# First modulation of a diffusion trunk: weights by pairs of feature blocks, three projection blocks beside them

## The chip, the cores and the metric

The kernel runs on one core of one Trainium2 chip. The metric is device time in microseconds (us) of one execution; lower is better. The engines are named as the profile names them: PE (TensorE, matrix products), PEld (its weight loads), DVE (VectorE), ACT (ScalarE), POOL (GpSimd) and SP (SyncE, which issues most loads). An engine works through its own instructions in a fixed order, and so does the queue of loads on SP.

## The reference

One sample, 512 latent tokens and 256 context tokens, 1024 features, two layers. The change lies in the very beginning of layer 0: the modulation vectors are computed from the conditioning, the tokens are normed and modulated, and the first input projection starts.

```python
silu_c = jax.nn.silu(c)
silu_cc = jax.nn.silu(c_ctx)
m_l = (silu_c @ w_mod[i] + b_mod[i])[:, None, :]       # w_mod[i]: 1024 x 6144
m_c = (silu_cc @ w_mod[i] + b_mod[i])[None, None, :]
sh1, sc1, g1, sh2, sc2, g2 = jnp.split(m_l, N_MOD, axis=-1)
hl = modulate(x, norm1_g[i], sh1, sc1)                 # rmsnorm(x) * (1 + sc1) + sh1
hc = modulate(ctx, norm1_g[i], csh1, csc1)
z  = h @ a_w_in                                        # 1024 -> 1440, for hl and for hc
# then two kinds of attention on parts of z, output projection, MLP; layer 1: Hyena, MLP
```

Only sh1 and sc1 (the first 2048 of 6144 columns of w_mod) are needed for the first projection. The other four parts are computed later in the background.

## The kernel before

Activations are kept transposed: features on the 128 partitions, in KD = 8 blocks, tokens along the free axis (`xnT`, `hl`). To reach near float32 precision, an operand is split into a rounded part and the rest (`hi`, `lo`; `split_w` does that to weights with one ACT and one DVE instruction), and a product is three matmuls (`mm3`: hi x hi, L109; hi x lo, L110; lo x hi, L111). One output block of the projection for the 512 latent tokens is thus 8 x 3 matmuls into one PSUM tile `sm`. The pool of those tiles (psB) has four buffers; the larger `big` tiles (psA) have two.

**Set-up** (`build`, L1297 to L1321). `conditioning` makes the silu of both conditioning vectors. `mod_start` (L272) loops over the eight blocks k of 128 input features: it loads a token tile of x (only for k < 4), then rows k*128 to k*128+127 of w_mod, columns 0 to 2047, as one load of 1 MiB with rows of 8 KiB (`wm`, three buffers). `norm0` norms the token tile and turns it with PE into xnT. Four matmuls (L289) add the block's product to one PSUM tile, in which row 32n+v holds columns 512n to 512n+511 for vector v (latent or context). The sum over k is complete only after the last load. `part` loads the weights of the first two output blocks of a_w_in (columns 672 to 927) in two halves. `vectors` (L225) loads biases and gains over the ACT queue and turns them into columns (`Acol`, `Bcol`, `Ccol`). `mod_finish` (L324) copies the sums out, turns them with four transposes (L331) and makes shift and scale columns `shsc`. `modulate0` (L344) then computes for each of the eight feature blocks hi on ACT (L349), the unrounded product on DVE (L351, one buffer `m0t`) and lo on DVE (L352). `context0` (L294) loads, norms and turns the two context tiles into `xcT`.

**Input projection** (`attn_in`, L457). Twelve output blocks follow each other: four of the grouped queries (`gq`, blocks j = 0 to 3, latent tokens only), then keys, values and the latent-attention parts, most of them for latent and context tokens. Blocks 0 and 1 run side by side over k. After each gq block, ACT takes the square (L515) and a scaled copy `gq0` (L517; one buffer), and DVE rotates it (L436 to L439). Block 0 stays in gq0 until it has been split for two heads (L723, L724). `context` modulates the context tokens. The generator `hidden` runs the filter network of layer 1 in between. After each block `block_done` calls `tick(3)`.

**Background.** `mod_chunks` (L354) computes the remaining four parts of the modulation on DVE: for each part eight loads of 512 KiB (`modw`, three buffers), eight multiply-adds (L372, L374), a transpose (L377) and a sum (L378). One step runs per tick, 37 steps in all, and the results are needed after the attention.

**Order.** A scheduler orders the instructions of each engine and of the SP queue when the program is built. It keeps their order in the program as priority, but lets a later instruction go first where it expects an earlier one to be still waiting. `keep_in_program_order` fixes an instruction in place. Tiles of a pool that is closed are overwritten by later pools as soon as their last reader is done. Pools grow from both ends of the memory (`side="right"`).

## Time and profile before

| what | value |
|---|---|
| median of 3 runs | 1534.65 us (1530.81 to 1539.14) |
| the profiled execution | 1532.22 us, span 1530.4 us |
| PE busy | 1431.5 us (94%) |
| DVE busy | 1107.9 us (72%) |
| ACT busy | 676.2 us (44%) |
| POOL busy | 294.1 us (19%) |
| DMA | 186.05 MB, mean 122 GB/s |

The span is the time from the first to the last instruction in the profiled execution. Busy shares are means over a span with several stages; the stage that is changed is its first 110 us. PE's busy time counts matmuls as overlapping intervals, so it is near the whole of a stage also where PE has to wait in between.

### The profile page before, as it was taken

Reading aid. Unit: us, or ns where it says so; the run is one execution under the profiler, and the core shown is the slowest. Engines: PE = TensorE matmul, PEld = TensorE weight load, DVE = VectorE, ACT = ScalarE, POOL = GpSimd, SP = SyncE. Lnnn points to the kernel's source line nnn. Section 1 sums busy time; section 2 is a strip of 40 time slices with the busy share of each in tenths; the row PEclk is TensorE's granted clock in tenths of the full one; section 3 lists DMA queues with packets and bytes.
Section 4 is the critical chain, followed back from the end, with each engine's and each line's share of the span. In section 5 each row is a group of like instructions: output and inputs, shape, how many; then the busy total and the mean of one; then the engine's idle time right before and its main releaser. Section 6 shows DMA issues by size and latency. Waiting matters only on the chain. (4 is left out here: it accounts for less than half of the span.)

```text
span 1530.4 us, 19652 instructions
## 1 busy us (share of the span) xinstructions
PE 1431.5 (94%) x7516; PEld 1191.7 (78%) x7516; DVE 1107.9 (72%) x1645; ACT 676.2 (44%) x1075; POOL 294.1 (19%) x245
## 2 busy tenths in 40 slices
PE   6798899999999998989999999999989999999998
PEld 2476687888887777878788977787778888888888
DVE  3999899877788989789765659897977434343454
ACT  3544587666644345345434444435234323132342
POOL 0000144322100322232220035634330000000001
PEclk8899899999999999999999999999999999999999
DMA  9655301211547655554334333321231232323331
GB/s 322 213 175 182 87 1 41 53 42 51 159 146 230 209 179 175 172 196 165 119 112 146 106 117 110 104 90 56 83 110 56 86 108 88 105 90 103 94 127 56
DMA packets 135435, 186.05 MB, mean 122 GB/s; under 512 B 16536, under 2 KB 118685, under 8 KB 132270
## 3 DMA queue, kind: packets, MB, share of 16 engines
q1 hardware_dynamic: 133168, 174.62, 35.3%
q0 software_dynamic: 1440, 9.70, 1.8%
q8 instruction: 59, 0.97, 0.3%
q10 hardware_dynamic: 734, 0.48, 0.1%
q14 instruction: 34, 0.28, 0.1%
HBM read 171.67 MB, written 10.49 MB: 119 GB/s over the span
## 5 line engine op out<-in xcount | busy, mean ns | idle before, releaser
L125 ACT CAST whi<-wraw 128x1024 fp32r<-128x1024 f32 (+2 forms) x203 | 195.9, 972 | 346.3 <-PE sm L110 311.0
L126 DVE TENSOR_TENSOR wlo<-wraw,whi 128x1024 fp32r<-128x1024 f32 (+2 forms) x195 | 235.8, 1212 | 121.1 <-ACT whi L125 108.3
L111 PE MATMUL sm<-h_hi,wlo 128*128 128x512 f32 (+1 forms) x720 | 273.6, 381 | 5.9 <-DVE wlo L126 5.9
L109 PE MATMUL sm<-h_hi,whi 128*128 128x512 f32 (+1 forms) x720 | 276.5, 387 | 2.6 <-ACT h_hi L425 1.7
L110 PE MATMUL sm<-h_lo,whi 128*128 128x512 f32 (+1 forms) x720 | 273.6, 381 | 0.7 <-DVE h_lo L426 0.7
L109 PE MATMUL sm<-mHhi,whi 128*128 128x512 f32 (+1 forms) x640 | 225.9, 354 | 2.4 <-ACT mHhi L169 2.3
L110 PE MATMUL sm<-mHlo,whi 128*128 128x512 f32 (+1 forms) x640 | 223.6, 350 | 3.4 <-DVE mHlo L172 3.4
L111 PE MATMUL sm<-mHhi,wlo 128*128 128x512 f32 (+1 forms) x640 | 223.2, 349 | 0.3 <-DVE wlo L126 0.2
L843 DVE SCALAR_TENSOR_TENSOR xT<-sm,mod,xT 128x256 f32<-128x256 f32 (+1 forms) x128 | 78.1, 614 | 131.8 <-PE sm L111 131.6
L111 PEld LDWEIGHTS sm<-h_hi,wlo 128*128 128x128 f32 x720 | 135.3, 188 | 34.6 <-DVE wlo L126 8.9
L109 PEld LDWEIGHTS sm<-h_hi,whi 128*128 128x128 f32 x720 | 134.8, 189 | 31.1 <-ACT h_hi L425 2.5
L110 PEld LDWEIGHTS sm<-h_lo,whi 128*128 128x128 f32 x720 | 135.8, 189 | 27.9 <-DVE h_lo L426 1.3
L110 PEld LDWEIGHTS sm<-mHlo,whi 128*128 128x128 f32 x640 | 121.7, 190 | 20.1 <-DVE mHlo L172 4.6
L109 PEld LDWEIGHTS sm<-mHhi,whi 128*128 128x128 f32 x640 | 121.6, 190 | 20.0 <-ACT mHhi L169 3.4
L111 PEld LDWEIGHTS sm<-mHhi,wlo 128*128 128x128 f32 x640 | 121.6, 190 | 16.7 <-DVE wlo L126 1.3
L647 POOL TENSOR_SCALAR prob<-prob,smx 128x768 f32<-128x768 f32 x64 | 60.4, 943 | 301.6 <-DVE smx L646 248.1
L374 DVE SCALAR_TENSOR_TENSOR modacc<-modw,silu,modacc 128x1024 f32<-128x1024 f32 x70 | 93.3, 1333 | 22.1 <-DMA modw<-in_w_mod 21.4
L937 POOL TENSOR_TENSOR Kout<-kE,kO 128x512 f32<-128x512 f32 x32 | 46.3, 1471 | 311.7 <-DVE kE L1073 190.9
L1257 POOL TENSOR_TENSOR facc<-facc,fsq 128x256 f32<-128x256 f32 x12 | 9.5, 792 | 386.7 <-ACT fsq L1255 386.7
L169 ACT CAST mHhi<-ms 128x512 fp32r<-128x512 f32 x64 | 39.6, 621 | 84.2 <-DVE ms L883 84.1
L1134 POOL TENSOR_TENSOR zx<-zx,zt 128x384 f32<-128x384 f32 x64 | 64.4, 1028 | 60.5 <-ACT zt L1132 59.3
L645 ACT ACTIVATE prob<-big,smx,qry 128x768 f32<-128x768 f32 x64 | 63.7, 996 | 12.3 <-DVE smx L643 9.6
(455 smaller groups left out, 2889.9 us busy)
## 6 DMA issues: line engine op xcount, KB each, us to landing
wraw<-in_mlp_w SPq DMA_DIRECT2D x67, 1024.0 KB
modw<-in_w_mod SPq DMA_DIRECT2D x80, 512.0 KB
wraw<-in_h_w_in SPq DMA_DIRECT2D x12, 1024.0 KB
wm<-in_w_mod SPq DMA_DIRECT2D x8, 1024.0 KB
kd<-Kout POOLq DMA_DIRECT2D x8, 1024.0 KB, 4.5
Kin<-kd SPq DMA_DIRECT2D x8, 1024.0 KB
wraw<-in_a_w_out SPq DMA_DIRECT2D x9, 512.0 KB
wraw<-in_a_w_in SPq DMA_DIRECT2D x4, 1024.0 KB
```

The costliest lines, as they stand in the source:

```text
L109: mm(ps, w.hi, x.hi, start=first, stop=False)
L110: mm(ps, w.hi, x.lo, start=False, stop=False)
L111: mm(ps, w.lo, x.hi, start=False, stop=last)
L125: pin(nc.scalar.copy(hi, r3))
L126: pin((lo_eng or nc.vector).tensor_tensor(out=lo, in0=r3, in1=f(hi), op=ALU.subtract))
L169: nc.scalar.copy(dst.hi, src)
L374: nc.vector.scalar_tensor_tensor(out=acc, in0=w, scalar=s, in1=acc, op0=ALU.mult, op1=ALU.add)
L645: nc.scalar.activation(out=p, in_=sf, func=AF.Exp, bias=sm[:, 1:2], scale=sc, accum_out=sm[:, 2:3])
L647: nc.gpsimd.tensor_scalar(out=p, in0=p, scalar1=sm[:, 3:4], scalar2=1.0, op0=ALU.mult, op1=ALU.mult)
L843: nc.vector.scalar_tensor_tensor(out=xt, in0=ps, scalar=gcol[:, d:d + 1], in1=xt, op0=ALU.mult, op1=ALU.add)
L937: tt = lambda e, o, x, y, op: e.tensor_tensor(out=o, in0=x, in1=y, op=op)
L1134: nc.gpsimd.tensor_tensor(out=t[:, o0:o0 + n], in0=t[:, o0:o0 + n], in1=b[:, i0:i0 + n], op=ALU.add)
```

## The change

Five things change, all within the first stage.

1. `mod_start` and `mod_finish` go; `mod_block(j)` takes their place, called for j = 0 to 3. Each call computes shift and scale of the feature blocks 2j and 2j+1 alone, over all 1024 input features. It loads 256 columns of shift and 256 of scale in eight loads of 256 KiB (two tiles `wm` of four loads; rows of 1 KiB). Four matmuls run beside each other on four groups of 32 PE columns, each with its own k; the second half adds to the first. So four partial sums lie at partitions 0, 32, 64, 96, and four small matmuls with `sel` (a matrix that picks partitions 0 mod 32 and 1 mod 32) add them up and turn them at once.
2. `modulate0` is called for two feature blocks at a time, right after their `mod_block`, and 18 matmuls follow: two feature blocks by three output blocks of three matmuls.
3. Three output blocks (j = 0, 1, 2) thus run along with the modulation instead of two after it. Their three PSUM tiles `ps3` are handed to `attn_in`, which computes only block j = 3 itself. The weights of blocks 2 and 3 come as one load `raw1` behind the first pair; block 3's half is split in `attn_in`.
4. All four token tiles of x are loaded first (`n0x` has four buffers instead of three), and `vectors` runs ahead of them.
5. The context loads and the first three background loads keep their place in the program, behind the modulation's weights; the pool `modp` of the background is opened after the set-up pool is closed, not before it.

```diff
-    def mod_start(self, tp, w0):
...
+    def mod_block(self, tp, j):
         nc, a = self.nc, self.a
+        both = self.big()
+        ps, pt = both[:, 0], both[:, 1, 0:8]
+        src = a["w_mod"][0].rearrange("(h k p) (m c) -> h p k m c", p=P, h=2, c=D)
+        for h in range(2):
+            w = tp.tile([P, 4, 2, 256], F32, name="wm", bufs=4)
+            for k in range(4):
+                nc.sync.dma_start(out=w[:, k], in_=src[h, :, k, 0:2, 256 * j:256 * j + 256])
+            for k in range(4):
+                nc.tensor.matmul(ps[32 * k:32 * k + 32], self.silu2[:, 4 * h + k], w[:, k].rearrange("p m c -> p (m c)"),
+                                 start=(h == 0), stop=(h == 1))
+        rows = tp.tile([P, 512], F32, name="modrow", bufs=2)
+        nc.vector.tensor_copy(rows[:, 0:256], ps[:, 0:256])
+        nc.scalar.copy(rows[:, 256:512], ps[:, 256:512])
+        for i in range(4):
+            nc.tensor.matmul(pt[:, 2 * i:2 * i + 2], rows[:, i * P:(i + 1) * P], self.sel, start=True, stop=True)
+        t = self.shsc[:, :, :, 2 * j:2 * j + 2]
+        pick = lambda ap, m: ap.rearrange("p (m j) -> p m j", m=m)[:, :, 2 * j:2 * j + 2].unsqueeze(1).broadcast_to([P, 2, m, 2])
+        nc.vector.tensor_tensor(out=t, in0=pt.rearrange("p (m e v) -> p v m e", m=2, e=2), in1=pick(self.Acol[:, 0:16], 2), op=ALU.add)
+        nc.vector.scalar_tensor_tensor(out=t[:, :, 1:2], in0=t[:, :, 1:2], scalar=1.0, in1=pick(self.n1g(0), 1),
+                                       op0=ALU.add, op1=ALU.mult)
     def context0(self, tp):
         for t in (4, 5):
+            xt = tp.tile([P, D], F32, name="n0x", bufs=4)
+            self.tc.keep_in_program_order(self.nc.sync.dma_start(out=xt, in_=self.a["ctx"][0, (t - 4) * P:(t - 3) * P]))
             self.norm0(tp, t, xt)
...
-    def mod_finish(self, tp):
...
-    def modulate0(self, h, v, x, tp, name):
-        nc = self.nc
-        for k in range(KD):
-            sh, g = self.shsc[v][:, k:k + 1], self.shsc[v][:, 8 + k:9 + k]
+    def modulate0(self, h, v, x, tp, name, ks=range(KD)):
+        nc = self.nc
+        for k in ks:
+            sh, g = self.shsc[:, v, 0, k:k + 1], self.shsc[:, v, 1, k:k + 1]
             nc.scalar.activation(out=h.hi[:, k], in_=x[:, k], func=AF.Identity, bias=sh, scale=g)
-            t = tp.tile([P, S], F32, name=name, bufs=1)[:, 0:x.shape[2]]
+            t = tp.tile([P, S], F32, name=name)[:, 0:x.shape[2]]
             nc.vector.tensor_scalar(out=t, in0=x[:, k], scalar1=g, scalar2=sh, op0=ALU.mult, op1=ALU.add)
             nc.vector.tensor_tensor(out=h.lo[:, k], in0=t, in1=f(h.hi[:, k]), op=ALU.subtract)
...
-                    nc.sync.dma_start(out=w, in_=a["w_mod"][l, k * P:(k + 1) * P, m * D:(m + 1) * D])
+                    load = nc.sync.dma_start(out=w, in_=a["w_mod"][l, k * P:(k + 1) * P, m * D:(m + 1) * D])
+                    if (l, m) == (0, 2) and k < mb:
+                        self.tc.keep_in_program_order(load)
...
-    def attn_in(self, hl, hc, w0, gp, ip, tp, context):
+    def attn_in(self, hl, hc, pss_w, raw1, gp, ip, tp, context):
         nc, a = self.nc, self.a
         w_in = a["a_w_in"][0]
         flat = lambda ps: ps.rearrange("p b n -> p (b n)")[:, 0:L]
-        ws = self.weights([w_in[:, i:j] for i, j in ((928, 1184), (1184, 1440), (384, 640), (640, 672), (0, 256), (256, 384))], KD)
+        cols = ((1184, 1440), (384, 640), (640, 672), (0, 256), (256, 384))
+        ws = self.weights([w_in[:, i:j] for i, j in cols], KD, self.fetch(w_in[:, 1184:1440], KD, 256))
         pss = self.sm()
         self.gq = []
         for c in range(2):
-            w = next(ws) if c else w0
-            both = [] if c else [self.sm() for _ in range(2)]
-            for k in range(KD):
-                for ps, wm in zip(both, w):
-                    self.mm3(ps, wm[:, k], hl[:, k], k == 0, k == KD - 1)
             for m in range(2):
                 j = 2 * c + m
-                if both:
-                    ps = both[m]
+                if j < 3:
+                    ps = pss_w[j]
                 else:
+                    w = self.split_w(raw1[:, :, 128:256])
                     ps = self.sm()
                     for k in range(KD):
-                        self.mm3(ps, w[m][:, k], hl[:, k], k == 0, k == KD - 1)
-                        if m and k == 2:
+                        self.mm3(ps, w[:, k], hl[:, k], k == 0, k == KD - 1)
+                        if k == 2:
...
+                with pool(name="setup", bufs=1, side="right") as tp:
+                    self.conditioning(tp)
+                    self.vectors(tp)
+                    hl, hc = (Split(hp0.tile([P, KD, n], F32R, name=nm + "_hi"), hp0.tile([P, KD, n], F32R, name=nm + "_lo"))
+                              for nm, n in (("hl", S), ("hc", C)))
+                    self.xcT = self.wp.tile([P, KD, C], F32, name="wraw")
+                    self.xnT = tp.tile([P, KD, S], F32, name="xnT")
+                    self.shsc = self.const.tile([P, 2, 2, KD], F32, name="shsc")
+                    for t in range(4):
+                        xt = tp.tile([P, D], F32, name="n0x", bufs=4)
+                        nc.sync.dma_start(out=xt, in_=self.rows(a["x"])[t])
+                        self.norm0(tp, t, xt)
+                    w3 = self.weight(a["a_w_in"][0][:, 672:928], KD, 256)
+                    raw1 = tp.tile([P, KD, 256], F32, name="wraw1")
+                    ps3 = [self.sm() for _ in range(3)]
+                    for j in range(4):
+                        self.mod_block(tp, j)
+                        if j == 0:
+                            nc.sync.dma_start(out=raw1, in_=a["a_w_in"][0][:, 928:1184].rearrange("(k p) n -> p k n", p=P))
+                            w3.append(self.split_w(raw1[:, :, 0:128], tp))
+                        self.modulate0(hl, 0, self.xnT, tp, "m0t", (2 * j, 2 * j + 1))
+                        for k in (2 * j, 2 * j + 1):
+                            for ps, w in zip(ps3, w3):
+                                self.mm3(ps, w[:, k], hl[:, k], k == 0, k == KD - 1)
+                    self.context0(tp)
                 mod_es = E(ExitStack())
                 self.modp = mod_es.enter_context(pool(name="modp", bufs=1))
                 self.mod_bufs = 3
                 self.bg = [self.mod_chunks(0, (2, 3, 4, 5), m0)]
-                with pool(name="setup", bufs=1, side="right") as tp:
-                    self.conditioning(tp)
-                    hl, hc = (Split(hp0.tile([P, KD, n], F32R, name=nm + "_hi"), hp0.tile([P, KD, n], F32R, name=nm + "_lo"))
-                              for nm, n in (("hl", S), ("hc", C)))
-                    self.xcT = self.wp.tile([P, KD, C], F32, name="wraw")
-                    raw, w0 = self.wp.tile([P, KD, 256], F32, name="wraw"), []
-                    def part(m):
-                        nc.sync.dma_start(out=raw[:, :, 128 * m:128 * m + 128],
-                                          in_=a["a_w_in"][0][:, 672 + 128 * m:800 + 128 * m].rearrange("(k p) n -> p k n", p=P))
-                        if m == 0:
-                            w0.append(self.split_w(raw[:, :, 0:128]))
-                    self.mod_start(tp, part)
-                    self.vectors(tp)
-                    fin = self.mod_finish(tp)
-                    next(fin)
-                    w0.append(self.split_w(raw[:, :, 128:256], pin=self.tc.keep_in_program_order))
-                    self.modulate0(hl, 0, self.xnT, tp, "m0t")
-                    next(fin)
-                    self.context0(tp)
                 ip_es = E(ExitStack())
                 ip = ip_es.enter_context(pool(name="ip", bufs=1, side="right"))
                 gp_es = E(ExitStack())
                 gp = gp_es.enter_context(pool(name="gp", bufs=1, side="right"))
                 with pool(name="inp", bufs=1) as tp:
-                    self.attn_in(hl, hc, w0, gp, ip, tp, lambda: self.modulate0(hc, 1, self.xcT, tp, "rpsh"))
+                    self.attn_in(hl, hc, ps3, raw1, gp, ip, tp, lambda: self.modulate0(hc, 1, self.xcT, tp, "rpsh"))
                 mod_es.close()
             self.pairs = []
             op_es = E(ExitStack())
```

Left out are the bodies of mod_start and mod_finish, which stand above, and two helper signatures.

## Rows read from the trace of the kernel before

**Rows 1.** Stretches: length, each engine's busy time, PE's granted clock, DMA share, GB/s.
```profile
0.00:42.00 42.00, 26.49 (x136) 11.31 (x136) 13.39 (x39) 15.05 (x23) 0.20 (x4) 0.85 0.91 330
42.00:130.00 88.00, 74.58 (x336) 53.01 (x336) 87.53 (x138) 43.07 (x63) 0.00 (x0) 0.95 0.64 201
130.00:190.00 60.00, 49.89 (x226) 37.77 (x227) 51.44 (x81) 30.67 (x50) 6.38 (x7) 0.86 0.34 98
```

**Rows 2.** Timeline, last weight block to first modulation: start, length, engine, line, operation.
```profile
37.85 1.94 PE L289 MATMUL sm<-wm,silu 128*32 128x512 f32 x8 [2.34 <-DMA wm<-in_w_mod]
...
41.90 0.55 DVE L351 TENSOR_SCALAR m0t<-xnT,shsc 128x512 f32<-128x512 f32 x1
```

**Rows 3.** Groups of DVE, 42 to 106 us: busy time, mean ns of one, idle.
```profile
L126 DVE TENSOR_TENSOR wlo<-wraw,whi 128x1024 fp32r<-128x1024 f32 x5 | 6.1, 1216 | 0.0
L352 DVE TENSOR_TENSOR hl_lo<-m0t,hl_hi 128x512 fp32r<-128x512 f32 x8 | 5.5, 689 | 0.1
L351 DVE TENSOR_SCALAR m0t<-xnT,shsc 128x512 f32<-128x512 f32 x8 | 4.4, 545 | 0.0
...
L322 DVE COPY wraw<-big 128x1024 f32<-128x1024 f32 x2 | 2.5, 1226 | 0.0
...
L311 DVE TENSOR_SCALAR n0n<-n0x,n0s 128x1024 f32<-128x1024 f32 x2 | 1.5, 752 | 0.0
...
L179 DVE SCALAR_TENSOR_TENSOR n0s<-n0s 128x1 f32<-128x1 f32 x2 | 0.3, 156 | 0.0
```

**Rows 4.** The DMA engines, 0 to 38 us.
```profile
DMA packets 4404, 12.22 MB, mean 322 GB/s; under 512 B 411, under 2 KB 2672, under 8 KB 3378
```

**Rows 5.** Stretches of 5 us in the load stage, columns as above.
```profile
0.00:5.00 5.00, 0.00 (x0) 0.00 (x0) 0.45 (x3) 1.16 (x1) 0.20 (x4) 1.00 0.65 192
...
10.00:15.00 5.00, 4.75 (x26) 2.53 (x18) 1.96 (x6) 2.46 (x4) 0.00 (x0) 1.00 1.01 417
15.00:20.00 5.00, 4.39 (x28) 2.41 (x29) 2.89 (x7) 2.46 (x4) 0.00 (x0) 1.00 0.80 254
...
35.00:40.00 5.00, 2.45 (x12) 0.20 (x8) 1.37 (x2) 1.04 (x1) 0.00 (x0) 0.50 1.06 363
```

**Rows 6.** A stretch that loads rows of 1 KiB alone (wraw of mlp_w).
```profile
1140.00:1145.00 5.00, 5.00 (x44) 5.00 (x43) 2.61 (x5) 0.71 (x2) 0.00 (x0) 1.00 1.05 355
```

**Rows 7.** Groups of DVE, 0 to 42 us.
```profile
L327 DVE COPY modrow<-sm 128x256 f32<-128x256 f32 x1 | 0.4, 425 | 2.3 <-PE sm L289 2.3
...
L337 DVE TENSOR_TENSOR shsc<-sm,Acol 128x16 f32<-128x16 f32 x2 | 0.3, 170 | 1.2 <-PE sm L331 1.2
L339 DVE SCALAR_TENSOR_TENSOR shsc<-shsc,Acol 128x8 f32<-128x8 f32 x2 | 0.2, 166 | 0.0
```

**Rows 8.** A group of PE in 0 to 42 us, and L289 in the timeline.
```profile
L331 PE MATMUL sm<-cst,modrow 128*128 128x128 f32 x4 | 1.1, 431 | 0.5 <-DVE modrow L327 0.5
```
```profile
25.86 1.06 PE L289 MATMUL sm<-wm,silu 128*32 128x512 f32 x8
```

**Rows 9.** Timeline of PE: end of output block 2, end of block 3.
```profile
77.49 0.62 PE L111 MATMUL sm<-hl_hi,wlo 128*128 128x512 f32 x2
...
83.49 0.39 PE L110 MATMUL sm<-hl_lo,whi 128*128 128x512 f32 x1
83.72 0.39 PE L111 MATMUL sm<-hl_hi,wlo 128*128 128x512 f32 x1
```

**Rows 10.** Timeline of SP: the first background loads.
```profile
34.47 10.72 SPq L369 DMA_DIRECT2D modw<-in_w_mod  x4
```

**Rows 11.** Timeline of ACT: square and scaled copy of blocks 0 and 1.
```profile
63.82 0.60 ACT L515 ACTIVATE sqS<-sm 128x512 f32<-128x512 f32 x1 [0.73 <-PE sm L111]
64.31 0.68 ACT L517 ACTIVATE gq<-sm,Ccol 128x512 f32<-128x512 f32 x1
...
74.02 0.69 ACT L517 ACTIVATE gq<-sm,Ccol 128x512 f32<-128x512 f32 x1 [1.65 <-DVE qs L724]
```

**Rows 12.** Waits of SP, 0 to 42 us; and a load in the chain that ended last.
```profile
SPq L285 <- DMA vC<-in_h_f_b: 5.8, 2, 5.5
```
```profile
1131.39 3.34 DMA wraw<-in_h_w_out
```

46 lines of the change are left out of this document (5 added, 41 removed).

## The prediction

> **What bounds the kernel now.** The change sits in the first 110 us of a span of 1530.4 us, so I read that stretch alone. First, the busy time by stretch [rows 1]. Up to 42 us VectorE (DVE) works 13.39 us and is idle for 28.6, while the DMA engines are 91% busy at 330 GB/s: this stage is bound by loads. From 42 to 130 us it turns over: DVE is busy 87.53 of 88 us, TensorE (PE) 74.58, the DMA 64%. From 130 to 190 us DVE is idle for 8.5 us. So the reader is to see two stages with two limits, loads and then DVE, and PE is the limit of neither although its share over the whole span is the largest.
>
> Second, where the first stage ends, in the timeline [rows 2]. The modulation's eighth and last weight block lets its matmuls start at 37.85; the sums are copied out and turned, and the first modulation op on DVE starts at 41.90. From the data to modulation it is 4.05 us, and nothing of the eight feature blocks can be modulated before.
>
> Third, what DVE does from 42 us on [rows 3]: the latent modulation (L351 and L352, 8 times each), weight splits (L126), context norm (L311, L322), rotations, and the background modulation (L374). The background steps are issued three per finished output block, and they are all needed later.
>
> **The change part by part.** The ledger is kept on DVE, because from 42 us on a microsecond is won only where DVE's idle time is removed. I take as milestone the moment at which all eight feature blocks are modulated and three output blocks' weights split.
>
> Before: 13.39 us of work by 42, of which 0.10 belongs to the first m0t; then 8 x 0.545 + 8 x 0.689 = 9.87 for modulation [rows 3], less that 0.10, and two more splits at 1.216 = 2.43. Together 25.6 us. DVE has no idle time after 42, so this content corresponds to 42 + 12.2 = 54.2 us; whatever else ran in between is work that need not be done again.
>
> After: the last weight pair must land first. Before moved 12.22 MB in its first 38 us [rows 4], 322 GB/s. Up to the last pair the new order moves x 2.10, the modulation's weights 8.39, two 1 MiB loads of a_w_in 2.10 (before: one) and constants 0.40, in all 12.99 MB: 40.3 us. Then the same 4.05 us to modulation (the four sum-and-turn matmuls with sel stand in for the four transposes of L331) and two feature blocks at 0.545 + 0.689: milestone at 40.3 + 4.05 + 2.47 = 46.9 us. Gain 54.2 - 46.9 = **7.3 us**.
>
> Bounds of that load time: the best and worst 5 us stretch of the load stage gave 417 and 254 GB/s [rows 5]. With 0.96 MB moved by 5 us, the last pair lands between 33.9 and 52.4 us, so this term lies between a gain of 13.7 and a loss of 4.8. I stay near the mean, because rows of 1 KiB alone, which is the new shape of these loads, ran at 355 GB/s [rows 6].
>
> Small DVE and ACT work: the row copy, addition and gain (L327, L337, L339: 0.425, 0.170, 0.166 each [rows 7]) run four times: 3.0 us instead of 1.1. The extra 1.9 us lie ahead of the milestone, where 25.6 + 1.9 = 27.5 us of work have 46.9 us: cost 0, and 1.9 if that cover were gone. ACT's four copies of the second half lie beside them.
>
> PE: the same 64 records of L289, 16 turning matmuls instead of 4 (0.43 each at the low clock [rows 8]), and 72 matmuls of three output blocks at 0.23 us pitch [rows 9] = 16.5 us, 12.4 of which now lie before the last pair lands. Per pair PE needs 2 x 1.06 + about 1.1 + 18 x 0.23 = 7.4 us at full clock, while a pair's 2.10 MB take 6.5 us: PE may be a little behind at the end. The bound is 0 to 4 us; I take **-1**, as a 1 MiB load (3.3 us) also lies between the pairs and lets PE catch up.
>
> Context: its two loads are now held behind the weights; their 1.05 MB land some 3.3 us after the last pair. Its norm costs DVE 0.75 + 1.23 + 0.6 us a tile [rows 3]. The first tile's start may fall into DVE's 4 us of waiting for the last sums: **+1.3** (0 to 2.6).
>
> Background: its first load was issued at 34.47 [rows 10] and now follows ctx, the rotary table and one a_w_in load (2.62 MB, 8 us), and its buffers share memory with set-up tiles that are freed only as the three blocks end. So DVE has only context work from 46.9 to about 53 us, and part of that waits for PE: a hole of 0 to 4 us, and I take **-1**. SP's queue is in order: a background load that waits for memory also holds the next a_w_in load behind it, but that is needed only after the fourth block.
>
> PE ahead of DVE: three blocks end at about 50 us, where before ends its third at 78.1 [rows 9]. That lead is not the gain. The next step on ACT (L517) needs gq0, which has one buffer that DVE's rotation frees: of the two blocks that PE had closed together by 63.8 the first had its turn at 64.31 and the second only at 74.02, released by DVE [rows 11]. PE will thus be held by DVE. What the lead does remove is some of the 8.5 us of DVE idleness between 130 and 190 us: **+2** (0 to 8.5).
>
> Sum: 7.3 - 1 + 1.3 - 1 + 2 = **8.6 us**. The profiled execution took 1532.2 (its span and 1.8 around it), which gives 1523.6; the median of the runs stands 2.4 higher, which gives 1526. I predict 1525.
>
> A rule that speaks against the change: eight loads of 1 MiB become 32 of 256 KiB. The Trainium skill, "DMA: Bandwidth & Descriptors", section "Bandwidth", asks to batch to 1 MiB or more, and its fit (2.0 us and bytes over 436 GB/s, measured on the GpSimd path) would give 2.6 us to each small load, 83 us for 32 end to end as an estimate from that page. No row shows loads of this size in a chain; the first rival prices it from rows.
>
> **The rivals.**
> A, slower: the small loads don't fill the DMA engines. Place: SP's queue, from 8 to 40 us. SP already waited 5.8 us there for small loads of another queue to land, and a 512 KiB load that was waited for alone took 3.34 us, 157 GB/s [rows 12]. At that rate the 8.39 MB take 53.4 us instead of 26.0, the milestone moves by 27, and 8.6 becomes a loss of 19: 1551. It turns slower by more than 0.5% where these loads fall below 8.39 / (26.0 + 16.3) = 198 GB/s. Against it: many loads are in flight together, and 355 GB/s for 1 KiB rows [rows 6].
> B, faster: PE's lead counts. Four blocks end at about 57 us instead of 84.1 [rows 9], and if DVE can push the background steps behind the attention's own work, as much as 26 us: 1506 to 1515. Against it: DVE is busy 87.53 of 88 us [rows 1], and the background steps stand ahead in the program.
> C, slower too, through PE: it falls to the low clock between the pairs, as between 35 and 40 us before (granted 0.50 of 2.4 GHz, so 1.2 [rows 5]). Then a pair costs PE 2 x 1.94 [rows 2] + 1.7 + 18 x 0.46 = 14 us against 6.5 of loading. The first pair is there at (2.10 + 1.05 + 2.10 + 0.40) / 0.322 = 17.5 us, and the milestone comes at 17.5 + 3 x 14 + 4.05 + 2.47 = 66 us, 12 later than 54.2: 1544. It decides from about 10 us a pair. Against it: the clock was full from 10 to 20 us while PE was busy for 9.1 of 10 [rows 5].
> D, it does not do what it says: the pairs are read early, but modulation still starts only after the last, because norms, Acol or PE's order hold it. All 9.87 us then follow 44.4: 54.3, no gain, 1532.
>
> **How the numbers follow.** Forecast 0.60 (1518 to 1532 by its bounds), A 0.08, B 0.12, C 0.08, D 0.12. A measurement of this kernel can tell about 0.5% (7.7 us) from no change. The forecast's 8.6 lies just beyond that, so some two thirds of its chance (0.40) go to faster and the rest to the same; B is faster (0.12); D is the same and a part of C, whose 14 us a pair is the dearest case; A and the rest of C, with the 0.02 of D that other small delays push over, are slower. Faster 0.52, same 0.34, slower 0.14. The range leaves out A, the dearest part of C and the best of B: 1508 to 1539.
>
> **What would show it.** In the profile after: the last L289-like matmul between 38 and 43 us; DVE idle up to 47 us about 19 us instead of 28.6, then busy without a break to 130; the third block's last matmul near 50; the fourth held by a free PSUM tile. Wrong if DVE has large holes between 45 and 60 us, if the DMA rate up to 40 us is under 250 GB/s, or if the granted clock is at the low level between 20 and 45 us.

## The result, and the profile after

| | before | after |
|---|---|---|
| median of 4 runs each, side by side | 1533.39 us (1530.81 to 1539.14) | 1555.88 us (1553.88 to 1558.20) |
| ratio, 95% interval | 1 | 1.0141 (1.0118 to 1.0165) |
| span of the profiled execution | 1530.4 us | 1556.4 us |

The change made the kernel 22 us slower, where 9 us less was forecast. The loss is early. The first matmul of the attention that reads the tile gK1hi is a good mark, since the instructions behind it are the same in all kernels. It starts at 209.00 us in the kernel before and at 239.12 in the kernel after (start, length, engine, line):

```profile
209.00 0.51 PE L738 MATMUL big<-gK1hi,qst 128*128 128x512 f32 x1
```
```profile
239.12 0.50 PE L722 MATMUL big<-gK1hi,qst 128*128 128x512 f32 x1
```

So the first part is 30.1 us longer, and the part behind the mark is 4 us shorter in this execution. The three stretches of [rows 1] look like this in the kernel after (length, busy time of PE, PEld, DVE, ACT, POOL, PE's granted clock, DMA share, GB/s):

```profile
0.00:42.00 42.00, 16.94 (x97) 12.45 (x97) 14.86 (x36) 15.46 (x23) 0.20 (x4) 1.00 0.68 217
42.00:130.00 88.00, 72.69 (x301) 46.67 (x301) 62.51 (x114) 33.32 (x52) 0.00 (x0) 0.84 0.55 174
130.00:190.00 60.00, 41.44 (x189) 31.83 (x190) 53.58 (x63) 20.27 (x26) 0.00 (x0) 0.80 0.64 193
```

DVE, on which the forecast kept its ledger, is idle for 88.0 - 62.5 = 25.5 us between 42 and 130; before it was 0.5. The DMA engines moved 217 GB/s in the first stage, before 330.

The loads of the weights were not slow; they stood still for long stretches. Stretches of 5 us, to be held against [rows 5]:

```profile
35.00:40.00 5.00, 3.70 (x36) 2.10 (x38) 3.27 (x4) 1.01 (x1) 0.00 (x0) 1.00 0.01 3
45.00:50.00 5.00, 5.00 (x23) 2.68 (x23) 3.73 (x8) 2.64 (x4) 0.00 (x0) 1.00 1.05 346
50.00:55.00 5.00, 5.00 (x24) 4.14 (x23) 0.92 (x2) 0.00 (x0) 0.00 (x0) 1.00 1.08 365
60.00:65.00 5.00, 3.50 (x18) 2.04 (x18) 3.64 (x12) 3.29 (x7) 0.00 (x0) 1.00 0.01 2
```

From 45 to 55 us the new loads of 256 KiB, nearly alone, ran at 346 and 365 GB/s; from 35 to 40 and from 60 to 65 nothing moved. The waits of SP from 0 to 80 us, as [rows 12] (line waited for: us in total, times, longest), name what held them:

```profile
SPq L449 <- DVE m0t L336: 20.7, 1, 20.7
SPq L282 <- PE big L284: 9.2, 1, 9.2
SPq L282 <- DMA wraw<-in_a_w_in: 6.5, 2, 5.0
...
SPq L140 <- DMA n0x<-in_x: 3.8, 1, 3.8
```

L282 loads the modulation's weights, L449 the rotary table, L140 weights of the projection. Three holds, then: at the start SP waits for loads with which its own share no tile; later for PE to free a buffer of weights; last, for 20.7 us, for memory. The timelines show each. (The profile infers what a wait is for.)

First the start, on ACT, whose queue issues the vector loads that the change moved ahead (start, length, line, and in brackets the idle time and its releaser):

```profile
1.18 0.44 ACTq L234 DMA_DIRECT2D vA<-in_b_mod  x1
...
11.29 3.94 ACTq L246 DMA_DIRECT2D vC<-in_h_f_b  x6
...
18.32 0.26 ACTq L250 DMA_DIRECT2D vC<-in_a_k_norm_g  x1
18.64 1.06 ACT L312 ACTIVATE n0n<-n0x 128x1024 f32<-128x1024 f32 x1 [13.41 <-DMA wm<-in_w_mod]
```

25 small loads took ACT's queue from 1.18 to 18.58 us, and ACT's first work on a token tile stood behind them. Then PE:

```profile
15.32 0.41 PE L255 MATMUL big<-cst,vB 109*128 109x109 f32 x1 [9.76 <-DMA vC<-in_h_f_b]
...
38.17 3.62 PE L284 MATMUL big<-wm,silu 128*32 128x512 f32 x26
...
56.30 2.76 PE L284 MATMUL big<-wm,silu 128*32 128x512 f32 x18
...
66.82 0.95 PE L291 MATMUL big<-cst,modrow 128*128 128x2 f32 x8
```

The turning of the vectors (L255) stands ahead of the token norms and waits 9.8 us for loads; the norms' transposes end at 38.2, and only then come the first modulation matmuls. The second half of the pairs (L284 at 56.30) stands on PE behind the products of the first two, from 48 us on; the last pair's sums are turned at 66.82. And DVE and SP:

```profile
72.40 0.69 DVE L337 TENSOR_TENSOR hl_lo<-m0t,hl_hi 128x512 fp32r<-128x512 f32 x1
76.89 2.36 DVE L126 TENSOR_TENSOR wlo<-wraw,whi 128x1024 fp32r<-128x1024 f32 x2 [3.80 <-ACT whi L125]
...
84.91 0.80 DVE L894 TENSOR_SCALAR prj<-sm,Ccol 64x512 f32<-64x512 f32 x1 [5.02 <-PE sm L969]
85.64 0.73 DVE L359 TENSOR_SCALAR modacc<-modw,silu 128x1024 f32<-128x1024 f32 x1
```

```profile
72.36 0.33 SPq L449 DMA_DIRECT2D ropet<-in_k_rope  x1
72.74 16.39 SPq L354 DMA_DIRECT2D modw<-in_w_mod  x5
```

The eighth feature block is modulated at 73.1 (forecast 46.9). Its product has read xnT by 72.3; that frees the memory, the rotary table and the first background load leave at 72.4 and 72.7 (the background's before at 34.47, [rows 10]), and DVE's first background step is at 85.64. In the kernel before it did eight such steps between 44 and 65 us, among the modulation's own; the first and the last of them there:

```profile
44.09 0.75 DVE L372 TENSOR_SCALAR modacc<-modw,silu 128x1024 f32<-128x1024 f32 x1
...
62.46 2.61 DVE L374 SCALAR_TENSOR_TENSOR modacc<-modw,silu,modacc 128x1024 f32<-128x1024 f32 x2
```

### The profile page after: what moved, and what is told of

It reads as the page before. It is cut to its first block, busy times and chain, and to the rows that moved or that the text cites. A ratio compares the mean times of both kernels' runs of the same rounds, so it can differ in the third digit from the quotient of the medians.

```text
span 1556.4 us, 19751 instructions
## 1 busy us (share of the span) xinstructions
PE 1438.1 (92%) x7544; PEld 1201.7 (77%) x7544; DVE 1108.5 (71%) x1652; ACT 677.1 (44%) x1078; POOL 293.6 (19%) x245
```

## The experiments

**Theory** after this reading: three causes add up: T1, the start (vectors), T2, memory (the background held), and T3, PE's order (a pair's weights behind the products of the pairs ahead). **Rivals**: that any one of them is all of it; later, that mending them brings nothing, as something else holds the stage. Each experiment gives the median time and its ratio to the kernel before, run beside it, with a 95% interval; 0.001 of the ratio is 1.5 us. The ratio is taken over all runs and can differ from the quotient of the medians by up to 0.0012. "The mark" is the start of the gK1hi matmul.

**1. Vectors late**: on the changed kernel, `vectors` behind the token tiles.

```diff
-                    self.vectors(tp)
...
                         self.norm0(tp, t, xt)
+                    self.vectors(tp)
```


> Changed kernel with the loads and turns of biases and gains (vectors) moved back behind the four token tiles; nothing else. Profiles so far: before 1530.4 us span, after 1556.4. Theory 1 (start): 25 small loads stand first on ACT's queue, each waits for a semaphore that an earlier large load holds, ACT reaches the first square at 18.64 us instead of 5.64, and PE's first modulation matmul moves to 38.17; the weight buffers are full by then and the DMA engines idle from 33 to 41. If so, the first square is at about 6, the first modulation matmul before 26, the last pair has landed at 42 to 46 instead of 57, the last feature block is modulated at 52 to 60 instead of 73, and the span is 1538 to 1544. Theory 2 (memory hold): the rotary table's load waits for the last reader of xnT and holds SP's queue, so the background starts late; this stays, so if it is the main cause the span is 1550 or more. Theory 3 (PE's order: product matmuls of one pair ahead of the sums of the next): the last modulation stays at least 10 us behind the last pair's landing.

1547.78 us, ratio 1.0096 (1.0065 to 1.0128): 0.0045, or 7 us, won. The first modulation matmuls come at 27.71 instead of 38.17, yet the last feature block is modulated only at 66.2, and SP still waits for memory:

```profile
SPq L449 <- DVE m0t L336: 17.9, 1, 17.9
```

So 10.5 us at the front became 6.9 at the end of the modulation; in between stands PE's order. The mark comes at 231.04, 8.1 us earlier; the span, 1545.3 us, is just above the 1538 to 1544 of theory 1.

**2. Memory alone**: a tile is reserved so that the weights `wm` lie where the next pools come first, and `xnT`, which is read to the end, lies above.

```diff
+                    tp.tile([P, 4, 2, 256], F32, name="wm", bufs=4)
                     self.xnT = tp.tile([P, KD, S], F32, name="xnT")
```


> Changed kernel with the buffers wm laid at the low end of the set-up pool, xnT above them; instructions as in the changed kernel. The rotary table's tile then lies over wm, whose last reader is PE's sum of the third pair, not over xnT, whose last reader is the last modulation. Theory 2: the rotary load goes at 56 to 60 us instead of 72.36, background loads directly behind, DVE's 9 us of holes between 73 and 85 and part of its holes between 50 and 72 fill, span 1545 to 1550. Theory 1: the first 57 us stay as they are (first modulation matmul at 38, last pair at 57), so most of the loss remains. If the hold costs nothing, span within 3 us of 1556.

1558.78 us, 1.0164 (1.0134 to 1.0195): nothing won. The background loads do move, from 72.74 to 63.03, but DVE's first background step comes no earlier (87.1, in the changed kernel 85.6), since on DVE it stands behind the step L894 that waits 5.0 us for PE. Theory 2 had 1545 to 1550.

**3. Both together.**


> Both edits: vectors behind the token tiles, and wm at the low end of the pool. If the two causes are separate, the gains add: 1556 less about 16 less about 8 gives 1532, no slower than the kernel before by more than 0.5%. If one hides the other (the rotary load is late only because the last pair is late), it is no more than 3 us better than the better of the two alone.

1541.01 us, 1.0046 (1.0023 to 1.0070): the ratio is 0.005, or 7.7 us, under that of experiment 1, with intervals that overlap. The traces do not show that the memory gave this. The background's loads start at 60.0 instead of 65.9, but up to 130 us DVE does the same in both executions: the last modulation ends at 66.2 in both, the first background step is at 77.4 and 76.9, the idle time is 43.8 and 44.1 us. The mark is 1.4 us earlier (experiment 1, then 3):

```profile
231.04 0.51 PE L722 MATMUL big<-gK1hi,qst 128*128 128x512 f32 x1
```
```profile
229.64 0.50 PE L722 MATMUL big<-gK1hi,qst 128*128 128x512 f32 x1
```

The other 3.3 us of the 4.7 between the two spans come behind the mark, where both run the same instructions. So the hold on memory has a price of 1.4 us in the trace; whether it is the cause of the rest is not shown.

**4. The kernel before with early vectors**: there `vectors` moves ahead of `mod_start`.


> Kernel before with one part of the change alone: vectors ahead of the token tiles and weight blocks. Theory 1 with cover: the first square moves from 5.6 to some 18 us here too and the norms end at about 38 instead of 26, but modulation waits for the eighth block at 38 anyway, and the large weight loads do not depend on norms; so 0 to 5 us slower than before (1530 to 1536 span). If early vectors cost by themselves (loads held by semaphores), the last block lands at 48 or later and the span is 1540 or more.

1538.06 us, 1.0029 (1.0005 to 1.0053). The same move costs the old kernel some 4 us: its last modulation weights are issued at 34.33 instead of 26.99. Its whole stage comes 5.0 us later (first modulation at 46.90 instead of 41.90), as the last weights do, and its mark 6.2 us later (215.21), not much less than the 8.1 us of experiment 1.

**5. Order alone**: on the changed kernel, pair j + 1's weights and sums stand ahead of pair j's products.

```diff
+                    self.mod_block(tp, 0)
                     for j in range(4):
-                        self.mod_block(tp, j)
...
                         self.modulate0(hl, 0, self.xnT, tp, "m0t", (2 * j, 2 * j + 1))
+                        if j < 3:
+                            self.mod_block(tp, j + 1)
                         for k in (2 * j, 2 * j + 1):
```


> The changed kernel with one difference: the weights and sums of pair j+1 stand in the program ahead of pair j's 18 product matmuls, not behind them. Everything else, the early vectors too, stays. Theory (the start is late because of the 25 vector loads ahead; PE's order is a second, smaller cause that matters at the end): the first matmul on modulation weights stays at about 38, but the last pair's no longer wait behind 36 product matmuls (48.0 to 56.3 in the changed kernel), so the last modulation comes some 5 to 8 us before 71.8, and the time falls by at most that: 1548 to 1554. Rival (PE's order is the main cause): the last modulation falls to under 58 and the time under 1542. Rival (only the background's loads count, which are held by memory): the time stays within 2 us of the changed kernel's 1556 unless those loads move from 72.7 us as well.

1551.64 us, 1.0104 (1.0061 to 1.0147); the last pair's sums are turned at 64.17 instead of 66.82:

```profile
64.17 0.95 PE L291 MATMUL big<-cst,modrow 128*128 128x2 f32 x8
```

The last modulation ends at 68.7, not 73.1, and the mark comes 3.4 us earlier (235.75): a second, smaller cause, as expected.

**6. All three.**


> The kernel with late vectors and with the modulation's weights low in memory (1541.0 us), and in it the order of the kernel before this one: weights and sums of the next pair ahead of this pair's products. Theory (three causes that add: late start, PE's order, memory): the last modulation comes near 52 instead of 62 to 64, the background loads near 52 instead of 60, and the time falls by 5 to 9 us, to 1532 to 1536, level with the kernel before the change. Rival (once the start and the memory are mended, DVE's later holes are set by the fourth block and the order of the background steps): within 2 us of 1541.

1535.18 us, 1.0012 (0.9989 to 1.0034): level with the kernel before. The last modulation ends at 55.3, the background loads start at 49.6. From the changed kernel the four steps run 1.0141, 1.0096, 1.0046, 1.0012, together 20 of the 22 us lost. The three edits together thus account for nearly all of the loss, and the sum is clear of the noise. How it is split is not: each interval overlaps the next, and the ratios (start 7 us, memory 8, order 5) and the marks (239.12, 231.04, 229.64, 217.82: start 8.1, memory 1.4, order 11.8) divide it differently. The order alone moved the mark by 3.4 us (experiment 5), on top of the other two by 11.8, so the causes do not simply add.

The forecast's gain stays missing. At the mark this kernel is even 8.8 us behind the kernel before, and what lies behind the mark takes 4.3 of that back: in the profiled executions of all kernels with the change that part was 0.3 to 10.4 us shorter than before (1321.4 us). No run took apart why; a level total thus does not mean a level first stage. In experiment 6 PE works through the pairs without a gap, 6.9 to 7.3 us each (the stretches between the turns of the sums):

```profile
28.99:36.27 7.28, 7.28 (x31) 0.77 0.87 273
36.27:43.17 6.90, 6.90 (x42) 1.00 1.05 344
43.17:50.29 7.12, 7.12 (x43) 1.00 1.05 363
```
(columns: length, PE's busy time, granted clock, DMA share, GB/s)

**7. Vectors over GpSimd's queue**, first on the changed kernel, then on experiment 6.

```diff
-        q = nc.scalar
+        q = nc.gpsimd
```


> The changed kernel with one difference: the 25 vector loads stay at the front of the program, but go over GpSimd's queue instead of ACT's. Theory (it is not that vectors come first, but that they and the large loads share ACT's and SP's semaphores, so that each small load waits for a large one): the token norms end near 25 to 27 instead of 39.5, ACT is free from the start, the first modulation matmul comes at 22 to 28, and the gain on the changed kernel is at least the 8 us that late vectors gave: 1540 to 1548. Rival (the front of the program itself is what counts: PE and DVE wait for the vectors because they stand first): the norms still end near 38 and the time stays within 3 us of 1556.

> As the last kernel, but the 25 small vector loads go over GpSimd's DMA queue instead of ACT's. Theory (ACT's small loads wait for semaphores that large loads of SP hold, and SP's loads wait for theirs): SP's 46 or so first loads then run without a break, the first modulation matmuls come near 18 instead of 25 to 27, the last pair lands at 40 to 43, all eight feature blocks are modulated by 48, and the time is 1522 to 1530, as the forecast had it. Rival (the loads are bound by bytes, as in the forecast's bound of 254 GB/s, and the semaphores are no cause): the last pair lands as in the kernel beside it, at 45 to 50, and the time is within 2 us of that kernel's.

On the changed kernel: 1544.89 us, 1.0063 (1.0035 to 1.0091), some 12 us won without a move in the program. ACT starts on the tokens at 5.91 instead of 18.64, but PE does not: its wait at L255 ends no earlier than before.

```profile
5.91 1.06 ACT L312 ACTIVATE n0n<-n0x 128x1024 f32<-128x1024 f32 x1 [0.72 <-DMA n0x<-in_x]
```
```profile
16.15 0.42 PE L255 MATMUL big<-cst,vB 109*128 109x109 f32 x1 [10.63 <-DMA vB<-in_final_g]
```

So both readings hold a part: the queue they share with large loads, and their place ahead of everything on PE. The norms end at 32.9, not at 25 to 27.

On experiment 6 the theory missed: 1543.28 us, 1.0061 (1.0040 to 1.0082), 7.5 us slower than with ACT's queue. The weights are issued no earlier (last at 42.5, there 40.3). In its profile the order built for DVE puts two weight splits ahead of the last token norm, PE's granted clock is 0.77 from 20 to 42 us (there 0.92), and the last modulation ends at 66.3; which of these made it slower was not tried.

**8. Is it the third block, or the products at all, that slow the pairs?** On experiment 6: all 72 products behind the pairs in the program, or the third block's 24.

```diff
-                            for ps, w in zip(ps3, w3):
+                            for ps, w in zip(ps3[:2], w3):
                                 self.mm3(ps, w[:, k], hl[:, k], k == 0, k == KD - 1)
+                    for k in range(KD):
+                        self.mm3(ps3[2], w3[2][:, k], hl[:, k], k == 0, k == KD - 1)
```


> The kernel with late vectors, the modulation's weights low in memory and the next pair's sums first (1535.2 us), and in it all 72 product matmuls behind the four pairs in the program, so that they only fill PE's waits. Theory (with the start and the memory mended, PE sets the pace: a pair took it 6.9 to 7.3 us without a gap, 18 products of 0.23 us among them, and the last of the eight feature blocks was modulated at 55.3): the last modulation comes with the loads, at 49 to 51, and the time falls by 3 to 6 us, to 1529 to 1532, the first version faster than the kernel before. Rival (PE's blocks are what DVE waits for after the modulation, and they only come later): the last modulation moves forward, but the first rotation stays at 61.6 or comes later, and the time is 1535 or more.

> The same kernel (1535.2 us) with only two of the three output blocks beside the pairs, the third's 24 product matmuls behind all pairs. Theory (PE sets the pace of the pairs): each of the three periods up to the last sum is 6 x 0.23 = 1.4 us shorter, the last modulation ends near 51 instead of 55.3, and the time is 1531 to 1533. Rival (the third block beside them costs nothing, since DVE's later work is the limit): within 2 us of 1535.

1544.52 us, 1.0076 (1.0050 to 1.0102), and 1538.86 us, 1.0033 (1.0013 to 1.0054). Both miss the theory. With all products last, the built order mixed them in between the weights' matmuls anyway, and the last modulation went to 62.2: no test of the pace. With two blocks it ended at 56.0, nearly unmoved, but in that execution the first sums were turned 2.65 us later (31.64, in experiment 6 28.99), so the three periods up to the last turn took 20.0 us instead of 21.3: 1.3 us shorter, not 4.2. The first rotation on DVE (the first step after a finished block) came 3.7 us later (65.3, in experiment 6 61.6). DVE waited there for the context's transposes, which stand on PE behind the third block's products:

```profile
62.99 2.36 DVE L327 COPY wraw<-big 128x1024 f32<-128x1024 f32 x2 [3.33 <-PE big L322]
```

The median rose by as much, but the intervals overlap; the rival (within 2 us of 1535) missed too.

**9. Context earlier, first pair earlier**, on experiment 6: the context's norm behind the last pair's sums; then also the first 1 MiB of projection weights behind the first pair.

```diff
                             self.mod_block(tp, j + 1)
+                        if j == 2:
+                            self.context0(tp)
...
-                    self.context0(tp)
```


> The kernel with late vectors, the modulation's weights low in memory and the next pair's sums first (1535.2 us); in it the context's norm moves in the program to right behind the last pair's weights and sums, ahead of the last two pairs' products. Its loads keep their place on SP's queue. Theory (the first rotation of the first output block sets DVE's start into its long stretch; it stands on DVE behind the context's two copies, and these wait for transposes that PE does behind all products): the transposes run before 55 instead of 58.2, DVE does the context in its waits for PE, the first rotation comes at 58 to 60 instead of 61.6, DVE's idle time up to 64 us falls by 2 to 4 us from 28.5, and the time is 1531 to 1533. Rival (PE sets the pace, and 32 transposes among the pairs delay the blocks by what they save): within 2 us of 1535.

> The same as the last, and the first 1 MiB of the projection's weights is loaded behind the first pair's modulation weights, not ahead of them. Theory (PE works through the pairs without a gap at 7.1 us each, so all that is left to win is an earlier first pair, now 24 to 29): the first pair's sums are turned at 25 to 27 instead of 29, all later steps move by as much, and the time is 2 to 4 us under the last kernel's, 1528 to 1531: the forecast's gain appears only here. Rival (the start is set by the token norms up to 22.4 and the small vector loads, not by the weights): under 1 us of difference.

1543.85 us, 1.0052 (1.0031 to 1.0073), and 1537.11 us, 1.0027 (1.0008 to 1.0046): both missed. The context is done by 59.2, as wanted, but now ACT modulates it (eight instructions, 59.2 to 63.2) ahead of the weight split on which DVE waits 5.0 us, and the first rotation comes at 66.5. (The profiled execution of the first of these took 1537.2, among the shortest of its runs, so the profile does not show all of its loss.) In the second, the first sums are turned at 28.8: as in experiment 6 (28.99) and not at 25 to 27, but 2.6 us earlier than in the first (31.38), whose first token tile also came 1 us later. Its median is 6.7 us under that of the first (by the ratios 3.8, with intervals that overlap): a difference more like the theory's (2 to 4) than the rival's (under 1), though neither time was met. The two executions do not say what sets the start.

**10. Products left out**, to see what the pairs do with PE free.

```diff
                             for ps, w in zip(ps3, w3):
-                                self.mm3(ps, w[:, k], hl[:, k], k == 0, k == KD - 1)
+                                if k in (0, KD - 1):
+                                    self.mm3(ps, w[:, k], hl[:, k], k == 0, k == KD - 1)
```


> The kernel with late vectors, the modulation's weights low in memory and the next pair's sums first (1535.2 us), with 18 of the 24 product matmuls of the third block left out (feature blocks 1 to 6 of it, so block 2's output is incomplete): 4.1 us less work for PE, some 1 us a pair. Theory (PE sets the pace): the sums are turned every 6 us instead of 7.1, the last modulation ends at 52 to 53 instead of 55.3, the first rotation comes near 58 instead of 61.6, and the time is 1531 to 1533. Rival (loads, and the chain sum, copy, turn, shift and scale on PE, DVE and ACT, give the pace): last modulation within 1 us of 55.3, time within 2 us of 1535.

> The same kernel with 54 of the 72 product matmuls of all three blocks left out (feature blocks 1 to 6), 12.4 us less work for PE in the pairs. Theory (PE sets the pace): the pairs follow the loads, the last modulation ends at 48 to 50, the first rotation comes at 54 to 56, and the time falls by 5 to 8 us, to 1527 to 1530: what the forecast wanted, had PE been free. Rival (DVE has nothing else to do there, since the background's loads start only behind the set-up, so its waits only move): the modulation ends early, but the time stays above 1532.

1535.90 us, 1.0002 (0.9984 to 1.0020), and 1533.39 us, 0.9994 (0.9977 to 1.0011). With 18 products gone the last modulation ended at 52.8 and the first rotation came at 58.4, both as the theory of PE's pace had it, and the time did not follow. With 54 gone the modulation ended at 52.6 and no earlier, and the first rotation came at 61.3; PE, with less to do, was at a granted clock of 0.75 from 42 to 64 us (in experiment 6 at 1.00). Both marks are 2.7 us earlier (215.15 and 215.08). So PE's pace delays the modulation by some 2.5 us and the mark by 2.7 of the 8.8 us: a part of the missing gain, too small for the medians to show, and not all of it.

**11. Background early**, on experiment 6: its pool opens ahead of the set-up's, its loads are not held in place, and `wm` and `n0x` have three buffers to make room.

```diff
-                    if (l, m) == (0, 2) and k < mb:
-                        self.tc.keep_in_program_order(load)
...
+                self.modp = mod_es.enter_context(pool(name="modp", bufs=1))
+                self.mod_bufs = 3
                 with pool(name="setup", bufs=1, side="right") as tp:
```


> The kernel with late vectors, the modulation's weights low in memory and the next pair's sums first (1535.2 us), and in it the background's pool opened ahead of the set-up's, as in the kernel before the change, and its first loads no longer held in their place; to make room, the modulation's weights have three buffers instead of four and the token tiles three. Theory (the forecast's gain was real, but it was given back because DVE had nothing to do between 42 and 64 us, 7.6 us idle, while the kernel before filled that time with background steps): DVE's first background step comes before 55 instead of at 65.6, its idle time from 0 to 130 us falls from 31.1 to 24 to 26, under the 29.1 of the kernel before, and the time is 1527 to 1531, the first version that beats it. Rival (DVE's idle time is no longer what counts once it is level with that of the kernel before; PE and the attention behind it are): the background comes early, and the time stays at 1533 or above.

1532.69 us, 1.0002 (0.9986 to 1.0018). The background starts early on DVE:

```profile
46.01 0.75 DVE L357 TENSOR_SCALAR modacc<-modw,silu 128x1024 f32<-128x1024 f32 x1
```

but DVE's idle time up to 130 us falls only to 29.3 us, where the theory had 24 to 26, and the time is level with the kernel before and not separable from experiment 6. The mark comes at 213.89, 3.9 us earlier than there and still 4.9 us behind the kernel before. No version beats the kernel before. Here are the changed kernel and experiment 6 from 0 to 130 us, and then experiment 11 in three stretches (columns as in the result; the third busy time is DVE's):

```profile
0.00:130.00 130.00, 89.63 (x396) 59.12 (x396) 77.38 (x150) 48.78 (x75) 0.20 (x4) 0.89 0.59 188
```
```profile
0.00:130.00 130.00, 96.80 (x472) 67.70 (x473) 98.92 (x177) 54.52 (x81) 0.20 (x4) 0.89 0.71 229
```
```profile
0.00:42.00 42.00, 26.83 (x146) 16.80 (x150) 20.99 (x49) 18.80 (x28) 0.20 (x4) 0.96 0.86 278
42.00:64.00 22.00, 20.81 (x117) 14.35 (x107) 15.51 (x31) 9.79 (x18) 0.00 (x0) 1.00 0.80 277
64.00:130.00 66.00, 51.97 (x243) 38.93 (x241) 64.17 (x101) 27.29 (x39) 0.00 (x0) 0.87 0.62 191
```

DVE's idle time up to 130 us, as 130 less its busy time, beside the mark and the span of the same execution:

| kernel | DVE idle, us | the mark, us later than before | span, us | first background step on DVE |
|---|---|---|---|---|
| 10, 18 products left out | 28.3 | 6.1 | 1536.2 | 62.6 |
| before | 29.1 | 0 | 1530.4 | 44.1 |
| 11, background early | 29.3 | 4.9 | 1526.9 | 46.0 |
| 10, 54 products left out | 29.8 | 6.1 | 1526.8 | 63.4 |
| 6, all three | 31.1 | 8.8 | 1534.9 | 65.6 |
| 4, before with early vectors | 34.0 | 6.2 | 1535.4 | 49.1 |
| 8, two blocks beside | 34.7 | 12.1 | 1538.2 | 69.3 |
| 9, context and first pair earlier | 36.1 | 12.4 | 1535.9 | 68.3 |
| 9, context earlier | 38.6 | 15.4 | 1535.4 | 72.4 |
| 7, vectors over GpSimd, on the changed kernel | 40.4 | 16.3 | 1542.9 | 72.3 |
| 8, all products last | 40.5 | 17.0 | 1541.9 | 75.5 |
| 7, vectors over GpSimd, on experiment 6 | 42.0 | 18.8 | 1542.7 | 76.0 |
| 3, late vectors and memory | 43.8 | 20.6 | 1540.6 | 77.4 |
| 1, late vectors | 44.1 | 22.0 | 1545.3 | 76.9 |
| 5, order alone | 48.4 | 26.7 | 1553.1 | 83.1 |
| after | 52.6 | 30.1 | 1556.4 | 85.6 |
| 2, memory alone | 54.0 | 31.3 | 1556.3 | 87.1 |

In all kernels with the change the mark follows the idle time one to one: it lies 4.7 to 7.4 us further behind the kernel before than the idle time. The span follows it too, but only to within some 7 us, as single executions scatter behind the mark; those of experiment 11 and of the 54 products are the shortest of their runs. So the forecast kept its ledger in the right currency, but the ledger lacked an entry. Up to the mark the kernel before and experiment 11 look like this:

```profile
0.00:209.00 209.00, 169.61 (x824) 118.44 (x825) 170.22 (x293) 105.13 (x166) 14.25 (x19) 0.91 0.55 179
```
```profile
0.00:213.89 213.89, 171.06 (x853) 125.38 (x853) 173.14 (x300) 106.28 (x169) 14.24 (x19) 0.90 0.55 175
```

Both have done 32 background steps by then. The 4.9 us are 2.9 more of busy DVE time and 1.9 more of idle time (40.7 against 38.8).

In experiment 11 DVE is idle for 21.0 us up to 42, 7.6 less than before [rows 1]: this is about the size of the forecast's gain, and it is there. Then come 6.5 us between 42 and 64 and 1.8 from 64 to 130, where the kernel before had 0.1 and 0.3. The two largest of its waits there (40 to 130 us), 6.2 of the 8.3 us:

```profile
DVE shsc L294 <- PE big L291: 3.4, 2, 1.7
DVE modrow L287 <- PE big L284: 2.8, 2, 1.4
```

DVE works in order, and its copy and its shift each wait for PE once per pair: 1.4 and 1.7 us each time. The kernel before sat through that chain once [rows 7]. That these waits are what took the gain is read from the profile; no run took them away.

## Why the prediction was wrong, point by point

**The step that failed first** is the change's fourth part, the vectors moved ahead. The prediction followed them as bytes (0.40 MB) but not as 25 instructions on ACT's queue, nor as three on PE ahead of the norms. The row that warned stood in its own text: SP waited 5.8 us for a vector load [rows 12]; it was used to price rival A instead. The first matmul on the modulation's weights came at 38.17, where the prediction (in rival C) had the first pair's data at 17.5. The price of the early vectors is 7 us on this kernel (experiment 1), about 4 on the old one (experiment 4).

**The last pair lands at 40.3.** This term carries the forecast, 7.3 of its 8.6 us. In the kernel after, the last of its loads was only issued at 49.3. The mean rate of [rows 4] was not the error in kind: unheld, the loads ran at 346 to 365 GB/s, and in experiment 6 the stage moved 288 GB/s up to 42 us, against 322 taken, which is worth 5 us. What failed is that loads were counted as free to run: with four buffers of weights they wait for PE (9.2 us), and PE waited for the norms.

**4.05 us from data to modulation, once.** In the kernel after, the last pair's weights stood on PE behind products of earlier pairs. PE's backlog was priced at 1 us, 4 at most, from 7.4 us a pair. The 7.4 was right (6.9 to 7.3 measured). What was missing is the start from which it counts: four pairs at 7.1 from 24 us end at 50 to 55, whatever the loads do. And the chain of sum, copy, turn and shift holds DVE once per pair, not once.

**Background, -1 of 0 to 4.** The set-up's memory was named ("freed only as the three blocks end"), and its price was taken as a hole of DVE of 1 us. Freeing the memory moved the mark by 1.4 us (experiment 3 against 1); the 7.7 us of the ratios are not traced to it. Starting the background early moved the mark by 3.9 (experiment 11 against 6), at the upper bound of the term. The eight steps that the kernel before did among its modulation had no row in the argument, although they filled DVE's time there after 42.

**Small DVE work, cost 0.** The extra 1.9 us of copies, additions and gains were put at nothing, as waits were to cover them. Up to the mark DVE is busy 2.9 us longer in experiment 11 and 3.1 in the kernel after, for the same background steps. What part of it waits would have covered no run took apart.

**Context +1.3, DVE idle recovered later +2.** Not separable. There is no sign of the +2: from 130 us to the mark DVE is idle for 13.2 us after, 11.4 in experiment 11 and 9.7 before. Moving the context (experiment 9) only moved the wait to ACT.

**The rivals.** A fell: the loads are fast where they run. The Trainium skill, "DMA: Bandwidth & Descriptors", section "Bandwidth", which spoke for it with its rule of 1 MiB or more, is not borne out here, for many loads in flight from SP: 346 to 365 GB/s at 256 KiB. C fell as stated: the granted clock was 1.00 up to 64 us. The 0.84 from 42 to 130 comes from later (0.79 from 64 to 130), when PE waits for DVE. B fell: three blocks ended near 75, not 50. D came nearest, and word for word: "norms, Acol or PE's order hold it". Its price, 1532, was wrong because it let modulation start at worst behind weights that land on time; norms and order also hold back the weights, through their buffers.

**The tests it set itself.** DVE's holes between 45 and 60 (0.92 us of work from 50 to 55) and the DMA rate below 250 GB/s (220 up to 40 us) both told it wrong; the clock did not. The range, 1508 to 1539, took the load term's bounds from rates alone, so no end of it held a stall. Its sums hold, except that 40.3 + 4.05 + 2.47 is 46.8 and not 46.9.

## What to carry to other kernels

When a step moves ahead, count its instructions on every queue and engine that it now stands in front of, and the small loads among them first. When a stage is cut into pieces that follow each other, cost each piece's chain of waits on every in-order engine, and ask which work filled those waits before: here it was the background, and its loads had been moved away by the same change. A load rate holds only while somebody frees the buffers. And where one stage is changed, compare the start of the same later instruction before the total, which adds the scatter of all that follows.

## What was not expected of the hardware

- A load can wait for another load with which it shares no tile, nor even a queue. SP's modulation weights waited 5.0 us for the projection's weights in the kernel after, and in experiment 6 for ACT's vectors vA and vB (2.1 and 1.7 us). What they share, semaphores by the look of the waits, no run took apart. 25 small loads of at most 0.6 us of issue each took 17.4 us on ACT's queue. Over GpSimd's queue the same loads left ACT free, but the last of the vB group was still not in before 16.15 us.
- The granted clock was 0.77 in a stretch in which PE never paused (28.99 to 36.27 us of experiment 6; 0.50, the level of 1.2 GHz, from 32 to 34), right after one in which it was busy for 6.4 of 11 us at the full clock (18 to 29 us): here the low level came after the gaps, not in them.
